# Spreading two products' additions, and fixing VectorE's and TensorE's order, in a decoder trunk on one core

## Chip, cores, metric

The kernel runs on one core of a Trainium2 chip. The metric is the time of one execution on the device in microseconds; the median of three runs of the kernel before is 2475.07 (2474.70 to 2475.67). Engines are named as in the profile: PE is TensorE's matmul, PEld its weight load, DVE VectorE, ACT ScalarE, POOL GpSimd, SP SyncE, whose queue issues most of the DMAs.

## Reference

Two layers: sliding-window attention, then a chunked spatial gating unit (SGU); behind each a conv-gated feed-forward (FFN). Every one of the four is wrapped in norms. The input is 1024 tokens of 1024 columns, in float32. The change touches the last matrix product of both FFNs and of the SGU, and the input projection of the FFN:

```python
def conv_gated_ffn(h, w_in, conv_w, conv_b, w_out):
    g, u = jnp.split(h @ w_in, 2, axis=-1)
    gp = jnp.pad(g, ((0, 0), (CONV_WIDTH - 1, 0), (0, 0)))
    g = conv_b + sum(conv_w[k] * gp[:, k:k + S] for k in range(CONV_WIDTH))
    return (jax.nn.gelu(g) * u) @ w_out
...
x = x + RMSNorm_post(sublayer(RMSNorm_pre(x)))
```

## The kernel before, in words

All matmuls are in float32 accuracy out of three passes over split operands: each operand is a high part, which ACT makes by a cast, and a low part, which DVE makes by a subtraction (`split`: L808 and L602, tile `osum`, eight buffers). A product of two split operands takes hi·hi, hi·lo and lo·hi.

`out_phase` (L908) ends each FFN and the SGU. The activations `ad` stand in DRAM, and the output is cut into four quarters c00, c01, c10, c11 (tiles `acc`). The quarters are computed by Strassen's seven products in Winograd's form, in two groups: g1 with products P1, P2, P6, P5, P7, P3, P4 of six steps each, and g2 with Q1, Q2, Q6, Q5, Q3, Q7, Q4 of four steps each in the FFNs and five in the SGU. One step is the split of two operands, and twelve matmuls of 128x512 (L880, four banks by three passes). The banks of the products change between `mm` and `ob`/`tb`. Between the products, DVE forms sums of operands (`sums1` to `sums4`) and adds finished products to the quarters; `u1`, `u2`, `u4` collect a running sum of three products (tile `u`, in `ww`) and add it to the quarters as they go.

What is left over of the inner dimension (two chunks) goes in by `part` (L253): its operands are split in Q1 (`chunk`, tile `ohl`, L1032 to L1036), six matmuls go into the bank of each token tile (L259), DVE adds the bank to `acc` (L262), ACT squares `acc` for the norm (L269, `junk`), and DVE multiplies `acc` by the norm's gain in place (L270). Such parts are `c11` in the last step of Q2, `c12` in the last of Q3, `c22` and `c21` in the last of Q7 and Q4. Behind the last three stand the norms.

The order of the work is given by the order of the code, by a scheduler that may move an instruction ahead of others of its engine, and by sections in which an engine keeps the order of the code (`tc.manual_schedule`). `run_products` (L890) strings the steps together. Of each step it first issues the splits of a step further ahead (`AHEAD`), then runs `what` (sums), the matmuls, `more` (a part) and `done` (additions). DVE keeps the code's order in the first 30 steps; from there to the end of the phase the scheduler has its choice on all engines.

In `ffn` (L1099) the input projections of the gated part go by pairs of columns in `pair_chain`: seven products of twelve matmuls (L748), tiles T1 to T4 and hhi/hlo, in three banks, with DVE's additions to `pu`, `u2` (L605) between them. The last pair's second chain is followed by `out_phase`, whose first matmuls the scheduler can place among those of the chain.

Of the kernel before, what the change touches and what calls it, by code (L numbers as in the profile page):

```python
# [37 lines left out]
def trunk_kernel(  # L38
# [27 lines left out]
    def mm_bank():  # L66
        return psum.tile([P, HALF], F32, name="mm", tag="mm")

    def out_bank():
        return pso.tile([P, HALF], F32, name="ob", tag="ob")  # L70
# [81 lines left out]
    def half_of(i):  # L152
        return slice(i * HALF, (i + 1) * HALF)
# [450 lines left out]
    def add_(out, a, b, eng=None):  # L604
        (eng or nc.vector).tensor_tensor(out=out, in0=a, in1=b, op=ALU.add)  # L605
# [111 lines left out]
    def chain(products, p1, u2, u4, a, b, c, out):  # L717


        go = iter(products)  # L720
        next(go)(a, True)
        nc.scalar.copy(out=p1, in_=a)
        yield
        next(go)(b, True)
        add_(u2, b, p1)
        yield
        next(go)(a, False)
        out(0, 0, a, None)
        yield
        next(go)(b, False)  # L730
        add_(u4, b, p1)
        yield
        next(go)(c, True)
        out(1, 1, c, u4)
        yield
        next(go)(b, False)
        out(0, 1, b, p1)
        yield
        next(go)(c, False)
        out(1, 0, c, u2)  # L740
        yield
# [11 lines left out]
    def pair_chain(ws, blocks, out):  # L753

        pu = gainp.tile([P, 2, HALF], F32, name="pu", tag="gpost")
        u2 = gainp.tile([P, 2, HALF], F32, name="u2", tag="gpre")[:, 0]
        a, b, c = out_bank(), mm_bank(), mm_bank()
        yield from chain([pair_product(w, t[1], blocks) for w, t in zip(ws, TERMS)], pu[:, 0], u2, pu[:, 1], a, b, c,
                         out)
# [28 lines left out]
    NPAIR = 6  # L788
# [100 lines left out]

    def run_products(products):  # L890

        steps = [s for p in products for s in p.steps()]
        n = 0

        def go(i0, i1):
            nonlocal n
            for i in range(i0, i1):
                while n < min(i + AHEAD[i >= 7 * NPAIR - 4] + 1, len(steps)):
                    steps[n][0]()
                    n += 1  # L900
                steps[i][1]()

        with tc.manual_schedule(engines={mybir.EngineType.DVE}):
            go(0, 5 * NPAIR)
        go(5 * NPAIR, len(steps))

    def out_phase(nchunk, ad, w_out, make_sub):
        with tc.tile_pool(name="junkp", bufs=2) as junkp:  # L908
# [2 lines left out]
    def out_phase_(nchunk, ad, w_out, make_sub, junkp):  # L911
# [33 lines left out]
        c = {(i, j): [sub.acc[4 * i + t][:, half_of(j)] for t in range(4)] for i in range(2) for j in range(2)}  # L945
# [33 lines left out]
        def both(*fs):  # L979
            def f(b):  # L980
                for x in fs:
                    x(b)
            return f

        def same(p):
            return lambda: p.banks


        def early(first):
# [5 lines left out]
        P5 = Product(g1, "P5", four0, both(g1.late, g1.sums4), less(c[0, 1], c[1, 0]))  # L995
        P7 = Product(g1, "P7", four1, None, both(from_(c[1, 1], c[0, 1]), lambda b: load((0, 1))))
        P3 = Product(g1, "P3", four0, None, add_to(c[0, 1]))
# [4 lines left out]
        g2 = Group(n2, [(xnp, "xn")] * 4 + [(work, "work")] * (n2 - 4), w_block(2 * NPAIR))  # L1002
        spare = halves(hs[0] + hs[1]), halves(soon), halves(hs[2] + hs[3])
        blocks = [("A", 0, 0, 0), ("B", 0, 0, 0), ("B", 0, 1, 1), ("A", 1, 0, 0), ("B", 1, 0, 1), ("B", 1, 1, 0),
                  ("A", 0, 1, 2), ("A", 1, 1, 2)]
# [41 lines left out]
        ww = []  # L1047
# [7 lines left out]
        def u2(b):  # L1055
            for t in range(4):
                add_(ww[t], b[t], ww[t])
                add_(c[1, 0][t], ww[t], c[1, 0][t])

        def u4(b):  # L1060
            for t in range(4):
                sub_(ww[t], b[t], ww[t])
                add_(c[0, 1][t], ww[t], c[0, 1][t])
                add_(c[1, 1][t], ww[t], c[1, 1][t])

        def c11(t, b):
            part(t, 0, b)
# [14 lines left out]
        Q1 = Product(g2, "P1", four0, both(g2.sums1, chunk), u1)  # L1082
        Q2 = Product(g2, "P2", same(Q1), g2.sums2, more=c11, first=False)
        Q6 = Product(g2, "P6", four1, g2.sums3, u2)
        Q5 = Product(g2, "P5", four0, g2.sums4, u4)
        Q3 = Product(g2, "P3", four1, more=c12)
        Q7 = Product(g2, "P7", four0, None, c22)
        Q4 = Product(g2, "P4", same(Q7), more=c21, first=False)
        run_products(seq + [Q1, Q2, Q6, Q5, Q3, Q7, Q4])
        return sub.h  # L1090

    def run(gen, *background):
        for _ in gen:
            poke()
            for b in background:
                next(b, None)


    def ffn(layer, h, make_sub):  # L1099
        nfc = DFF // P  # L1100
# [19 lines left out]
        with tc.tile_pool(name="gsp", bufs=2) as gsp, tc.tile_pool(name="cvp", bufs=4) as cvp:  # L1120

            def part(j, half, parts):
                if half == 0:
                    new_gs(j)
                    gu[j] = in_unit(fw_in[layer], j * P)
                    uu[j] = in_unit(fw_in[layer], DFF + j * P)
                ps = in_proj(gu[j], h, half, parts)
                yield
                nc.scalar.copy(out=gs[j][:, 2 + half * HALF:2 + (half + 1) * HALF], in_=ps)
                cv = cvp.tile([P, HALF], F32, name="cv", tag="cv")  # L1130
                conv(j, cv, half * HALF, HALF)
                ps = in_proj(uu[j], h, half, parts)
                yield
                nc.vector.tensor_tensor(out=cv, in0=ps, in1=cv, op=ALU.mult)
                nc.sync.dma_start(out=ad[j][:, half_of(half)], in_=cv)

            for j in range(2):
                run(part(j, 0, 2))
            flush()
            blocks = Blocks(h)  # L1140
            bs = blocks.steps()
            for j in range(2):
                run(part(j, 1, 2), bs, bs, bs)
            for j in range(2, 2 * PLAIN_FFN):
                for half in range(2):
                    run(part(j, half, 1), bs, bs, bs, bs, bs)
            run(bs)

            def gate(j, first=False):

                cv = {}

                def cv_of(i, jj):
                    return cv[i, jj] if first and i == 0 else cv[i][:, half_of(jj)]

                def g_out(i, jj, ps, rest):
                    dst = gs[j + i][:, 2 + jj * HALF:2 + (jj + 1) * HALF]
                    if rest is None:
                        nc.scalar.copy(out=dst, in_=ps)
                    else:  # L1160
                        add_(dst, ps, rest)
                    if first and i == 0:
                        cv[i, jj] = cvp.tile([P, HALF], F32, name="cv", tag="cv")
                        conv(j, cv[i, jj], jj * HALF, HALF)
                    elif i != jj:
                        cv[i] = work.tile([P, S], F32, name="cv", tag="work")
                        conv(j + i, cv[i], 0, S)

                def u_out(i, jj, ps, rest):
                    dst = cv_of(i, jj)  # L1170
                    if rest is not None:
                        add_(rest, ps, rest)
                        ps = rest
                    nc.vector.tensor_tensor(out=dst, in0=ps, in1=dst, op=ALU.mult)
                    if first and i == 0:
                        nc.sync.dma_start(out=ad[j][:, half_of(jj)], in_=dst)
                    elif i != jj:
                        nc.sync.dma_start(out=ad[j + i], in_=cv[i])

                return g_out, u_out  # L1180

            j0 = 2 * PLAIN_FFN
            g_out, u_out = gate(j0, True)
            gw = pair_unit(fw_in[layer], j0 * P, (j0 + 1) * P, True)
            new_gs(j0)
            new_gs(j0 + 1)
            gc = first_chain(gw, blocks, g_out, cvp.tile([P, HALF], F32, name="p1", tag="cv"))
            next(gc)
            next(gc)
            uw = pair_unit(fw_in[layer], DFF + j0 * P, DFF + (j0 + 1) * P, True)  # L1190
            uc = first_chain(uw, blocks, u_out, cvp.tile([P, HALF], F32, name="p1", tag="cv"))
            next(uc)
            for _ in gc:
                pass
            for _ in uc:
                pass

            for j in range(j0 + 2, nfc, 2):
                g_out, u_out = gate(j)
                gw = pair_unit(fw_in[layer], j * P, (j + 1) * P)  # L1200
                new_gs(j)
                new_gs(j + 1)
                run(pair_chain(gw, blocks, g_out))
                uw = pair_unit(fw_in[layer], DFF + j * P, DFF + (j + 1) * P)
                run(pair_chain(uw, blocks, u_out))

        return out_phase(nfc, ad, fw_out[layer], make_sub)

# [259 lines left out]
```

## Time and profile before

| | us |
|---|---|
| median of three runs | 2475.07 |
| the profiled execution, whole | 2475.61 |
| its span in the trace | 2473.9 |
| PE busy | 2414.4 (98%) |
| DVE busy | 1851.3 (75%) |
| ACT busy | 1052.4 (43%) |
| POOL busy | 341.8 (14%) |

Times of the trace count from the start of the span. The first FFN's last product runs from about 780 to 1000, the SGU's from 1560 to 1790, the second FFN's from 2225 to the end. Busy shares are means; a wait in the views of waits is put down to the release that came last.

### The profile page before, as it was taken

The page shows a single profiled execution, that of the slowest core. Times are in us where ns is not written, and L with a number is a line of the kernel's source. Part 1 is how long each engine was busy: PE and PEld are TensorE (multiplying, and loading weights), DVE is VectorE, ACT ScalarE, POOL GpSimd, SP SyncE. Part 2 cuts the span into 40 slices and gives each one's busy share as a digit, 9 for nine tenths or more (in the row PEclk, how much of TensorE's full clock was granted, in tenths as well). Part 3 has the DMA queues.
Part 4 walks back from the last instruction along what each step waited for, and adds up shares of the span by engine and source line. Part 5 has one row for each costly group of instructions (what it writes and reads, how often), then busy time and mean ns, then how long its engine had stood idle before and what let it go on. Part 6 is the DMA issues. An engine that isn't in the chain of part 4 may idle for free.

```text
span 2473.9 us, 33879 instructions
## 1 busy us (share of the span) xinstructions
PE 2414.4 (98%) x12488; PEld 2029.6 (82%) x12488; DVE 1851.3 (75%) x3224; ACT 1052.4 (43%) x1957; POOL 341.8 (14%) x442
## 2 busy tenths in 40 slices
PE   9999989999999999999999999999999999999997
PEld 8777778888887787789998888788797888887886
DVE  5766799767767887886667776787887767767877
ACT  4654565333333444443333333444453333334443
POOL 1000010000000111100027777202110000001011
PEclk9999999999999999999999999999999999999999
DMA  7322142222224952433334444974222222238642
GB/s 238 65 47 56 44 154 69 77 87 92 69 94 154 260 156 69 153 107 99 94 97 148 135 141 150 295 220 81 94 95 85 68 94 86 76 103 259 192 86 102
DMA packets 269943, 296.34 MB, mean 120 GB/s; under 512 B 30447, under 2 KB 195665, under 8 KB 269778
## 3 DMA queue, kind: packets, MB, share of 16 engines
q1 hardware_dynamic: 257106, 271.11, 34.2%
q0 software_dynamic: 12672, 23.07, 5.7%
q8 instruction: 98, 1.61, 0.3%
q14 instruction: 67, 0.55, 0.1%
HBM read 211.29 MB, written 65.01 MB: 112 GB/s over the span
## 4 chain that ended last, share of the span: by engine, by line
PE 84%; DVE 10%; DMA 3%; issue 2%; ACT 1%; POOL 0%; SPq 0%; DVEq 0%; POOLq 0%; ACTq 0%
PE mm L748 27%; PE ob L748 11%; PE mm L880 11%; PE mm L148 7%; PE mm L1286 6%; PE ob L880 3%; PE ob L259 3%; PE tb L880 3%; PE ob L1286 2%; DVE osum L602 2%; PE tb L1416 2%; DMA raw<-ad 2%; PE mm L259 1%; DMA raw<-in_ffn_w_out 1%; PE tb L473 1%
## 5 line engine op out<-in xcount | busy, mean ns | idle before, releaser
L748 PE MATMUL mm<-T,wsum 128*128 128x512 f32 x2496 | 597.4, 392 | 5.4 <-ACT wsum L710 4.2
L748 PEld LDWEIGHTS mm<-T,wsum 128*128 128x128 f32 x2496 | 468.3, 189 | 105.8 <-ACT wsum L710 6.0
L880 PE MATMUL mm<-osum 128*128 128x512 f32 x1644 | 390.1, 391 | 8.1 <-ACT osum L808 4.4
L880 PEld LDWEIGHTS mm<-osum 128*128 128x128 f32 x1644 | 306.6, 188 | 76.0 <-DVE osum L602 5.8
L808 ACT CAST osum<-raw 128x512 fp32r<-128x512 f32 x372 | 215.8, 619 | 305.2 <-PE mm L880 103.7
L602 DVE TENSOR_TENSOR osum<-raw,osum 128x512 fp32r<-128x512 f32 x372 | 242.9, 690 | 84.2 <-ACT osum L808 84.0
L748 PE MATMUL ob<-hhi,wsum 128*128 128x512 f32 x864 | 287.3, 393 | 0.1
L710 ACT CAST wsum<-sums 128x512 fp32r<-128x512 f32 x208 | 127.7, 621 | 292.8 <-DVE sums L602 164.1
L1401 POOL TENSOR_SCALAR vn<-vn,mv,rv 128x128 f32<-128x128 f32 x192 | 193.3, 1018 | 73.9 <-DMA vn<-vd 26.2
L602 DVE TENSOR_TENSOR wsum<-sums,wsum 128x512 fp32r<-128x512 f32 x208 | 142.8, 690 | 68.0 <-ACT wsum L710 67.5
L748 PEld LDWEIGHTS ob<-hhi,wsum 128*128 128x128 f32 x864 | 161.7, 188 | 35.7 <-ACT wsum L710 3.4
L748 PE MATMUL ob<-hlo,wsum 128*128 128x512 f32 x432 | 168.7, 390 | 0.0
L710 ACT CAST wsum<-raw 128x512 fp32r<-128x512 f32 x156 | 96.5, 620 | 163.7 <-PE mm L748 140.3
L605 DVE TENSOR_TENSOR pu<-mm,pu 128x512 f32<-128x512 f32 x110 | 75.7, 688 | 105.4 <-PE mm L748 105.3
L880 PE MATMUL ob<-osum 128*128 128x512 f32 x480 | 133.8, 393 | 13.8 <-DVE osum L602 13.8
L148 PE MATMUL mm<-hhi,whi 128*128 128x256 f32 (+1 forms) x416 | 136.0, 329 | 0.7 <-ACT hhi L211 0.7
L148 PE MATMUL mm<-hlo,whi 128*128 128x256 f32 (+1 forms) x416 | 135.7, 327 | 0.0
L148 PE MATMUL mm<-hhi,wlo 128*128 128x256 f32 (+1 forms) x416 | 134.6, 325 | 0.2 <-DVE wlo L125 0.2
L880 PE MATMUL tb<-osum 128*128 128x512 f32 x480 | 132.5, 389 | 0.0
L748 PE MATMUL mm<-hhi,wsum 128*128 128x512 f32 x384 | 126.7, 391 | 0.0
L1116 DVE SCALAR_TENSOR_TENSOR cv<-gs,cw,cv 128x1024 f32<-128x1024 f32 (+1 forms) x100 | 115.7, 1157 | 14.1 <-issue 8.3
L880 PEld LDWEIGHTS ob<-osum 128*128 128x128 f32 x480 | 88.9, 188 | 38.0 <-DVE osum L602 20.2
(257 smaller groups left out, 4526.6 us busy)
## 6 DMA issues: line engine op xcount, KB each, us to landing
raw<-in_ffn_w_in SPq DMA_DIRECT2D x88, 512.0 KB, 4.0
raw<-ad SPq DMA_DIRECT2D x80, 256.0 KB, 5.4
raw<-in_ffn_w_out SPq DMA_DIRECT2D x80, 256.0 KB, 5.7
ad<-cv SPq DMA_DIRECT2D x38, 512.0 KB, 3.2
raw<-in_sgu_w_in SPq DMA_DIRECT2D x28, 512.0 KB, 4.4
xs<-xt SPq DMA_DIRECT2D x24, 512.0 KB, 2.6
vn<-vd SPq DMA_DIRECT2D x48, 256.0 KB, 3.2
ads<-ut SPq DMA_DIRECT2D x24, 512.0 KB, 3.1
```

Source lines behind the costliest of these rows:

```text
L148: nc.tensor.matmul(ps[:, cs], a[:, k, :], b[:, k, cs], start=n == 0, stop=n == 3 * KC - 1)
L259: nc.tensor.matmul(ps, a, b[:, half_of(nh)], start=n == 0 and not begun, stop=n == end, skip_group_check=begun)
L602: (eng or nc.vector).tensor_tensor(out=out, in0=a, in1=b, op=ALU.subtract)
L605: (eng or nc.vector).tensor_tensor(out=out, in0=a, in1=b, op=ALU.add)
L710: nc.scalar.copy(out=t[:, 0], in_=src)
L748: nc.tensor.matmul(bank, x, y, start=first and n == 0, stop=n == 3 * H4 - 1, skip_group_check=True)
L808: nc.scalar.copy(out=t[:, 0], in_=src)
L880: nc.tensor.matmul(self.banks[t], u, v, start=self.first and g == 0 and m == 0, stop=last and self.more is None and m == 2, skip_group_che ...
L1116: nc.vector.scalar_tensor_tensor(out=cv, in0=gs[j][:, k + t0:k + t0 + n], scalar=tap_w(k, j), in1=cv, op0=ALU.mult, op1=ALU.add)
L1286: nc.tensor.matmul(bank[r][:, q * NQ:(q + 1) * NQ], x, y, start=first and q == 0 and m == 0, stop=m == 3 * H4 - 1, skip_group_check=True)
L1401: nc.gpsimd.tensor_scalar(out=vn[:, t, :], in0=vn[:, t, :], scalar1=mv[:, tt, 0:1], scalar2=rv[:, tt:tt + 1], op0=ALU.subtract, op1=ALU.mult)
L1416: nc.tensor.matmul(sv[:, t, :], vn[:, t, :], gws[(j + i) // 3][0], start=True, stop=True)
```

## The change

Three things. (1) `u2` and `u4` only update the running sum; its additions to the quarters, `plus_u`, are `what` of later products: one token tile in each of four steps of Q5 (to c10), Q3 (to c01) and Q7 (to c11). (2) DVE keeps the order of the code up to the last step of Q3: 61 of 70 steps in an FFN, 66 of 77 in the SGU. (3) The last `pair_chain` of the up-projection of each FFN keeps the code's order on PE.

```diff
     def run_products(products):
...
+        fixed = len(steps) - 2 * products[-1].group.n - 1
         with tc.manual_schedule(engines={mybir.EngineType.DVE}):
-            go(0, 5 * NPAIR)
-        go(5 * NPAIR, len(steps))
+            go(0, fixed)
+        go(fixed, len(steps))
...
         def u2(b):
             for t in range(4):
                 add_(ww[t], b[t], ww[t])
-                add_(c[1, 0][t], ww[t], c[1, 0][t])
 
         def u4(b):
             for t in range(4):
                 sub_(ww[t], b[t], ww[t])
-                add_(c[0, 1][t], ww[t], c[0, 1][t])
-                add_(c[1, 1][t], ww[t], c[1, 1][t])
+
+        def plus_u(i, j):
+
+            return lambda t: add_(c[i, j][t], ww[t], c[i, j][t]) if t < 4 else None
...
-        Q5 = Product(g2, "P5", four0, g2.sums4, u4)
-        Q3 = Product(g2, "P3", four1, more=c12)
-        Q7 = Product(g2, "P7", four0, None, c22)
+        Q5 = Product(g2, "P5", four0, both(plus_u(1, 0), g2.sums4), u4)
+        Q3 = Product(g2, "P3", four1, plus_u(0, 1), more=c12)
+        Q7 = Product(g2, "P7", four0, plus_u(1, 1), c22)
...
                 uw = pair_unit(fw_in[layer], DFF + j * P, DFF + (j + 1) * P)
-                run(pair_chain(uw, blocks, u_out))
+                with tc.manual_schedule(engines={mybir.EngineType.PE}) if j + 2 >= nfc else ExitStack():
+                    run(pair_chain(uw, blocks, u_out))
```

The changed code's lines count from one more behind L891 to four more at the end (L1035 is L1037). In the rows of the order below, the numbers behind a name are those of its buffer or tile.

DVE in the first FFN, before, around the c11 parts, which stand in the last step of Q2. `acc_7333` to `acc_7336` are the four token tiles of c11, `osum_8408` and `osum_8411` the operands of a step of Q6:

```order
L602 TENSOR_TENSOR osum_8389<-sums_7341,osum_8389 128x512
L262 TENSOR_TENSOR acc_7333<-mm_8256,acc_7333 128x512
L270 TENSOR_TENSOR acc_7333<-acc_7333,gpost_7263 128x512
L275 TENSOR_SCALAR ms_8759<-ss2_8451 128x1
L262 TENSOR_TENSOR acc_7334<-mm_8257,acc_7334 128x512
L262 TENSOR_TENSOR acc_7335<-mm_8258,acc_7335 128x512
L270 TENSOR_TENSOR acc_7334<-acc_7334,gpost_7263 128x512
L275 TENSOR_SCALAR ms_8790<-ss2_8465 128x1
L602 TENSOR_TENSOR osum_8408<-raw1_7275,osum_8408 128x512
L602 TENSOR_TENSOR osum_8411<-sums_7342,osum_8411 128x512
L262 TENSOR_TENSOR acc_7336<-mm_8259,acc_7336 128x512
L270 TENSOR_TENSOR acc_7335<-acc_7335,gpost_7263 128x512
```

The same place of the change, where `osum_8432` and `osum_8435` are Q6's third step and `acc_7336` to `acc_7339` the four tiles; `osum_8498` and `osum_8501`, Q6's last step, are the next row behind these:

```order
L602 TENSOR_TENSOR raw1_7278<-sums_7347,raw1_7278 128x512
L262 TENSOR_TENSOR acc_7336<-mm_8258,acc_7336 128x512
L270 TENSOR_TENSOR acc_7336<-acc_7336,gpost_7266 128x512
L262 TENSOR_TENSOR acc_7337<-mm_8259,acc_7337 128x512
L275 TENSOR_SCALAR ms_8758<-ss2_8453 128x1
L270 TENSOR_TENSOR acc_7337<-acc_7337,gpost_7266 128x512
L262 TENSOR_TENSOR acc_7338<-mm_8260,acc_7338 128x512
L275 TENSOR_SCALAR ms_8789<-ss2_8467 128x1
L270 TENSOR_TENSOR acc_7338<-acc_7338,gpost_7266 128x512
L262 TENSOR_TENSOR acc_7339<-mm_8261,acc_7339 128x512
L275 TENSOR_SCALAR ms_8832<-ss2_8481 128x1
L270 TENSOR_TENSOR acc_7339<-acc_7339,gpost_7266 128x512
```

Before, splits stand between the tiles, and two L262 ahead of the second L270. Now the four tiles follow each other, each with its L270 behind its own L262 and ahead of the next tile's, and no split lies between them.

ACT at the same place, before (L269 is the square, L808 the cast of a split):

```order
L808 CAST osum_8389<-sums_7341 128x512
L269 ACTIVATE junk_8443,ss2_8451<-acc_7333 128x512
L269 ACTIVATE junk_8457,ss2_8465<-acc_7334 128x512
L808 CAST osum_8408<-raw1_7275 128x512
L808 CAST osum_8411<-sums_7342 128x512
L269 ACTIVATE junk_8471,ss2_8479<-acc_7335 128x512
L269 ACTIVATE junk_8485,ss2_8493<-acc_7336 128x512
L808 CAST osum_8430<-raw1_7275 128x512
L808 CAST osum_8433<-sums_7343 128x512
L808 CAST osum_8496<-raw1_7275 128x512
```

ACT, the change:

```order
L808 CAST osum_8435<-sums_7346 128x512
L808 CAST osum_8498<-raw1_7278 128x512
L808 CAST osum_8501<-sums_7347 128x512
L808 CAST osum_8521<-sums_7344 128x512
L808 CAST osum_8524<-raw1_7278 128x512
L269 ACTIVATE junk_8445,ss2_8453<-acc_7336 128x512
L269 ACTIVATE junk_8459,ss2_8467<-acc_7337 128x512
L269 ACTIVATE junk_8473,ss2_8481<-acc_7338 128x512
L269 ACTIVATE junk_8487,ss2_8495<-acc_7339 128x512
```

The first two squares have moved behind eight more casts; the last four of these are of Q6's last step (`osum_8498`, `osum_8501`) and of Q5's first (`osum_8521`, `osum_8524`).

PE in the last up-projection of the first FFN, before (`T1` and `T3` are tiles of operands, `mm_7023` the bank of this half's product and `mm_7161` that of another):

```order
L748 MATMUL mm_7023<-T1_4435,wsum_7002 128x512 x2
L748 MATMUL mm_7023<-T1_4436,wsum_7002 128x512
L748 MATMUL mm_7023<-T1_4435,wsum_7002 128x512
L748 MATMUL mm_7161<-T3_4504,wsum_7147 128x512 x2
L748 MATMUL mm_7161<-T3_4505,wsum_7147 128x512
L748 MATMUL mm_7161<-T3_4504,wsum_7147 128x512
L748 MATMUL mm_7023<-hhi1_3741,wsum_7010 128x512
L748 MATMUL mm_7023<-hlo1_3742,wsum_7010 128x512
L748 MATMUL mm_7023<-hhi1_3741,wsum_7010 128x512 x2
```

PE there, the change:

```order
L748 MATMUL mm_7023<-T1_4436,wsum_7002 128x512
L748 MATMUL mm_7023<-T1_4435,wsum_7002 128x512 x2
L748 MATMUL mm_7023<-T1_4436,wsum_7002 128x512
L748 MATMUL mm_7023<-T1_4435,wsum_7002 128x512
L748 MATMUL mm_7023<-hhi1_3741,wsum_7010 128x512
L748 MATMUL mm_7023<-hlo1_3742,wsum_7010 128x512
L748 MATMUL mm_7023<-hhi1_3741,wsum_7010 128x512 x2
L748 MATMUL mm_7023<-hlo1_3742,wsum_7010 128x512
```

The four matmuls of T3 that stood between the last of T1 and the first of hhi, into another bank, are gone from there; T3's twelve now come further down, one after the other.

## Rows read from the trace of the kernel before

**Rows 1.** The page: busy us, share of the span, instructions.

```profile
PE 2414.4 (98%) x12488; PEld 2029.6 (82%) x12488; DVE 1851.3 (75%) x3224; ACT 1052.4 (43%) x1957; POOL 341.8 (14%) x442
```

**Rows 2.** Waits of PE, whole span: us in total, times, longest.

```profile
PE ob L880 <- DVE osum L602: 13.8, 15, 1.7
```

**Rows 3.** Waits of PE, 950 to 976 us, Q5 and Q3.

```profile
PE ob L880 <- DVE osum L602: 2.3, 2, 1.7
PE mm L880 <- DVE osum L602: 0.5, 1, 0.5
```

**Rows 4.** Timeline of DVE near Q6: start, us, what [idle before <- releaser].

```profile
936.42 0.69 DVE L262 TENSOR_TENSOR acc<-mm,acc 128x512 f32<-128x512 f32 x1 [0.39 <-PE mm L259]
937.96 0.69 DVE L270 TENSOR_TENSOR acc<-acc,gpost 128x512 f32<-128x512 f32 x1 [0.85 <-ACT junk L269]
...
938.64 0.68 DVE L262 TENSOR_TENSOR acc<-mm,acc 128x512 f32<-128x512 f32 x1
...
945.24 0.69 DVE L602 TENSOR_TENSOR osum<-raw,osum 128x512 fp32r<-128x512 f32 x1 [0.42 <-ACT osum L808]
```

**Rows 5.** Timeline of ACT, the same stretch.

```profile
937.21 0.63 ACT L269 ACTIVATE junk<-acc 128x512 f32<-128x512 f32 x1 [2.64 <-DVE acc L262]
...
950.55 0.61 ACT L808 CAST osum<-raw 128x512 fp32r<-128x512 f32 x1
```

**Rows 6.** Timeline of PE, Q6 of the first FFN and of the SGU.

```profile
941.66 1.52 PE L880 MATMUL ob<-osum 128*128 128x512 f32 x6
...
951.64 1.07 PE L880 MATMUL tb<-osum 128*128 128x512 f32 x4
...
1716.46 1.07 PE L880 MATMUL ob<-osum 128*128 128x512 f32 x4
```

**Rows 7.** Timelines, Q6 of the SGU: DVE, then ACT.

```profile
1711.58 0.69 DVE L602 TENSOR_TENSOR osum<-sums,osum 128x512 fp32r<-128x512 f32 x1
...
1713.62 0.62 ACT L808 CAST osum<-sums 128x512 fp32r<-128x512 f32 x1
...
1716.28 0.61 ACT L808 CAST osum<-sums 128x512 fp32r<-128x512 f32 x1
```

**Rows 8.** DMA issues: KB each, median us to landing.

```profile
raw<-ad SPq DMA_DIRECT2D x4, 512.0 KB, 4.6
```

**Rows 9.** Waits of PE, 980 to 1085 us, norms after the first FFN.

```profile
PE tb L210 <- DVE t L602: 2.9, 1, 2.9
PE ob L1286 <- DVE vlo L602: 1.6, 1, 1.6
PE mm L880 <- DVE acc L602: 1.1, 1, 1.1
```

**Rows 10.** Timelines, last up-projection: first FFN (PE, DVE), second (PE).

```profile
777.88 0.50 PE L748 MATMUL mm<-hhi,wsum 128*128 128x512 f32 x1
...
793.76 0.74 PE L880 MATMUL mm<-osum 128*128 128x512 f32 x2 [1.98 <-ACT osum L808]
...
777.14 0.69 DVE L605 TENSOR_TENSOR pu<-mm,pu 128x512 f32<-128x512 f32 x1 [2.50 <-PE mm L748]
...
788.95 1.28 DVE L1116 SCALAR_TENSOR_TENSOR cv<-gs,cw,cv 128x1024 f32<-128x1024 f32 x1
...
2237.77 0.74 PE L880 MATMUL mm<-osum 128*128 128x512 f32 x2 [1.90 <-ACT osum L808]
```

**Rows 11.** Stretches: us, busy us of each engine, granted clock, DMA, GB/s.

```profile
425.00:430.80 5.80, 3.38 (x12) 1.62 (x11) 5.80 (x9) 4.39 (x8) 0.00 (x0) 1.00 0.31 90
430.80:434.40 3.60, 3.60 (x10) 2.81 (x11) 3.41 (x7) 1.69 (x4) 0.00 (x0) 0.53 0.03 9
...
1062.30:1069.20 6.90, 5.66 (x15) 4.33 (x16) 6.90 (x10) 2.28 (x4) 0.00 (x0) 0.51 0.01 2
...
790.00:797.00 7.00, 5.02 (x22) 3.79 (x21) 3.51 (x6) 2.29 (x3) 0.00 (x0) 1.00 0.85 296
966.00:976.00 10.00, 7.70 (x33) 5.69 (x32) 8.47 (x15) 2.81 (x5) 0.00 (x0) 1.00 0.29 105
```

## The prediction

> **What bounds the kernel now.** I read the page first, for its busy shares [rows 1]. TensorE (PE) is busy for 2414.4 us, 98% of the span, and VectorE (DVE) for 75%, so the end is set by PE, and only what opens or closes a gap on PE counts. Second, the view of PE's waits, for who ends those gaps [rows 2]: the largest is "ob L880 <- DVE osum L602", 13.8 us in 15 waits, a matmul waiting for the low half of a split operand. Third, the same view for the stretch that the change aims at, Q5 and Q3 in the first FFN: 0.5 + 2.3 = 2.8 us [rows 3]. The same stretch of the SGU and of the second FFN prints the same two rows, so spreading the additions can win 8.4 us at the very most. Fourth, the timelines of DVE, ACT and PE around Q6, where the fixed order puts something new: [rows 4 to 6]. There the reader should see that the c11 parts' chains (L262, ScalarE's square L269, L270) begin at 936.42, a tile at a time, while PE goes on with Q6 at 941.66 without a gap.
>
> The profiled execution took 2475.61 us; the median of the runs is 2475.07. I add to the first and take off 0.5 at the end. About 5 us (0.2%) is what a measurement of this kernel can tell from no change.
>
> **1. The c11 parts, now in fixed order.** Before, each L262, L270 and split ran on DVE when it was ready: two tiles, then a split, then the rest. In the fixed order all four tiles stand in one row behind the low halves of Q6's third step, each L270 straight behind the L262 of its own tile, and the splits of Q6's fourth step stand behind all of them. L270 overwrites what the square reads, so DVE stands still until the square is done. One tile costs, from the start of one L262 to the start of the next, 938.64 − 936.42 = 2.22 us [rows 4]; without the tiny L275, which moves into the waiting time, 2.15. The square itself also moves: on ACT the four squares now stand behind the casts of Q6's last and Q5's first step. The second of those casts starts at 950.55 and takes 0.61 [rows 5]; it waits for PE's third step, which is not earlier than before.
>
> So: first square at 951.16; L270 follows 937.96 − 937.21 = 0.75 later and takes 0.61 at DVE's cadence: 952.5. Three more tiles, 3 × 2.15: 959.0. Then two low halves, 0.61 + 0.69: 960.3. PE needs them after the high passes of two steps, which the order interleaves, at 951.64 [rows 6]. PE stands for **8.7 us**; queued behind the four tiles on DVE are the splits of Q6's last and all of Q5's steps, and PE alone waits for those. The loads of Q5's operands on SP's and POOL's queues wait for buffers that come free as late as PE is, and are ahead of it by the same distance: nothing. The second FFN has the same order and the same durations: **8.7**. In the SGU one square is ahead of the casts of the step after: its first cast row is at 1713.62 and ends at 1714.23 [rows 7], the first L262 is done at 1714.6 (it starts behind the three additions that follow the low half at 1711.58: 1712.2 + 1.8 = 1714.0), its L270 at 1716.05. The second square waits for two more casts, of which the later starts at 1716.28, so the second L270 ends at 1718.3; two more tiles, 1722.6; two low halves, 1723.9. PE needs them at 1716.46 [rows 6]: **7.5 us**. Sum: 24.9. Bounds: nothing, if DVE stands while PE still has work (which would need the chain to be done by 950.3), and 4 × 2.22 + 1.3 = 10.2 in each phase.
>
> **2. The additions of U2 and U4, spread.** Taken out: 2.8 us in each phase [rows 3]. But in Q3 DVE must now do one acc addition and one sums4 addition ahead of each split. Two additions are 1.22, and cast and low half take 0.61 + 0.61 + 0.69 = 1.9 from the release of a buffer: 3.1 us of chain for a step of 2.72. That leaves 0.4 in each of four steps, and I put 0.9 on the step in which the four subtractions of U4 come as well: 2.5 per FFN phase, −0.3 each. The SGU's Q3 has one step more in which the splits can run ahead, so I put 0.95 there: −1.85. Together **−2.45**; bounds −8.4 (every gap gone) and +2.
>
> **3. Q1.** ACT's cast of Q1's second chunk (L1035) now stands ahead of the split casts of the next step. Its 512 KB load lands a median 4.6 us after issue [rows 8], and is issued only after the first chunk's subtraction. I estimate 0.4 in each FFN phase and nothing in the SGU: **+0.8**; bounds 0 and 4.6 × 2 less what lies beside, some +3.6.
>
> **4. The norms.** The additions of c10, c01 and c11 that left Q5 come later, into Q3 and Q7. Eight at 0.61 with four more of sums4 are up to 7 us of DVE work pushed towards the norms, where PE waits for DVE already [rows 9]: 2.9 + 1.6 + 1.1 after the first FFN. Part of it lies beside Q7 and Q4 (eight steps of 2.72). I take 2.4 us (four additions) as the most that arrives late, and 1.5, 1.0 and 0.5 as estimates in the three phases (after the second FFN PE's rest is short): **+3.0**; bounds 0 and 7.2.
>
> **5. The last up-projection in fixed order.** Removed are the gaps of 1.98 and 1.90 [rows 10], in which PE waits for the cast of an operand of P1 whose matmuls had been drawn into the chain. Put in their place: T1, the hi/lo twelve and T4 stand back to back. The twelve write T1's bank and wait for DVE's pu, which ran from 777.14 to 777.83; PE went on at 777.88 without a gap [rows 10] because four matmuls of T3 (0.91) stood between. They are gone from there: about 1.0 of new wait. At the second half the same wait comes behind a cv of 1.28 on DVE [rows 10]: 1.4 as an estimate. 2.4 against 1.9 is +0.5 each, **+1.0**; bounds −3.9 (no new gap) and +3.
>
> **6. The clock.** Where PE had worked 3.38 of 5.80 us, the next 3.60 ran at a granted clock of 0.53 [rows 11]; the longest such stretch is 6.90 us at 0.51 [rows 11]. That is 1.2 GHz in place of 2.4. In each new stall PE works far less than that (at most eight matmuls in 9 us). A stretch of 3.60 us at 0.53 loses 0.47 × 3.60 = 1.7; one behind each of three stalls is **+5.1**. Bounds: 0 and 3 × 0.49 × 6.90 = 10.1.
>
> The Trainium skill, "TensorE: Matmul & The Clock Gate", section "A second HAM failure mode: psum-queue depth-cycling", says that small, frequent idles between groups of matmuls are enough to make the clock fall and rise again and again; that speaks against part 2, which makes two large gaps into four or five small ones. By that rule Q3 would lose one more stretch in each phase, 3 × 1.7 = 5.1. Here the row 966 to 976 has PE at 7.70 of 10 us, with the gaps in it, at 1.00 [rows 11], so the trace of before does not bear it out.
>
> Sum: 2475.6 + 24.9 − 2.45 + 0.8 + 3.0 + 1.0 + 5.1 = 2508.0; on the scale of the median **2507.5**.
>
> **The rivals.**
> *The clock stays up.* The rest of the sum holds, without 5.1: 2502. For it: 1.98 us of idle at 793.76 left the clock at 1.00 [rows 10, 11].
> *More of the clock.* Each stall is followed by the long stretch, or the small gaps of Q3 drop it: +5.1 again, 2513. This is where the rule of the Trainium skill in part 6 would lead, if Q3 were the place.
> *The chain costs half.* The squares get in between the casts (ACT's order is a queue, but its casts may be released earlier), so that DVE's own cadence, 1.22 a tile, sets it: 4 × 0.93 = 3.7 less in each phase, and no clock: 2502 less 11, near 2491; if the first square also stands ahead of the casts, it starts 2.2 earlier (the first L262 would be done at 949.0), 2484.
> *Faster.* L270 of the fourth tile is through by 950.3, so PE never waits, and only the gains are left: part 2's −2.45, part 5 without new gaps −3.9, part 3's +0.8: 2475.1 − 5.5 = 2469.5. It decides at 950.3: the chain of four would have to begin near 941.7. Against it: the low halves of the third step, behind which it stands, start at 945.24 [rows 4].
> *No effect*, if the order of DVE were not the limit anywhere: 2475.
>
> **How the numbers follow.** The forecast, 2504 to 2511: 0.50. Clock stays up, 2498 to 2504: 0.22. More of the clock, 2511 to 2518: 0.12. Half the chain, 2482 to 2494: 0.08. Faster, 2470: 0.04. No effect or something near it: 0.04. From 2490 to 2515 lie the first two whole, about three quarters of the third and some of the fourth: a little over 0.8. Faster by over 0.2%: 0.03, since 2470 lies at that bound; within 0.2%: 0.05; slower: 0.92.
>
> **What would show it.** In the profile after: one wait of PE for "DVE osum L602" of about 8 us in each of the three phases, near Q6's fourth step; on DVE there four pairs of L262 and L270 in a row with an idle "<- ACT junk L269" ahead of each L270; on ACT the squares behind the casts; a granted clock of 0.5 right after the stall. In Q3, four or five gaps of about 0.5 in place of 1.70 and 0.60. No gap of 1.9 at the last up-projection, but some 2 us of waits for DVE's pu. I am wrong if PE passes Q6 without a wait of over 2 us.

## The result, and the profile after

The changed kernel takes 2507.34 us (2506.45 to 2508.29), the kernel before in the same session 2475.37: the ratio is 1.0130, with a 95% interval of 1.0117 to 1.0143. It is slower by 32 us. The forecast was 2507.5. The profiled execution took 2507.93 us, its span is 2506.2.

The page after, where [rows 1] stood:

```profile
span 2506.2 us, 33928 instructions
PE 2430.0 (97%) x12488; PEld 2035.8 (81%) x12488; DVE 1856.0 (74%) x3224; ACT 1052.3 (42%) x1957; POOL 338.8 (14%) x442
```

The number of matmuls is the same, and PE is *busy* for 15.6 us more than before, so part of the loss does not show as waiting. Two things are in these 15.6 us: matmuls at half the clock, which take longer, and matmuls that stand alone between two waits, which the trace counts at 0.5 to 0.8 us each, where one in a row takes 0.227. How much is the clock is worked out below.

The view of PE's waits, whole span (us in total, times, longest), where [rows 2] stood:

```profile
PE ob L880 <- DVE osum L602: 20.2, 15, 7.5
PE mm L880 <- DVE acc L262: 6.1, 4, 1.6
...
PE mm L880 <- DVE ms L275: 3.0, 2, 1.6
```

The longest wait for a low half went from 1.7 to 7.5 us, and two names are new, which PE's L880 did not wait for before: PE waits for the banks that L262 reads. (In the rows with "ms L275" the matmul also waits for L262, which ends just behind that small instruction's start.) Where they lie shows in DVE's timeline of the first FFN at Q6, columns as in [rows 4]:

```profile
946.97 0.69 DVE L602 TENSOR_TENSOR raw<-sums,raw 128x512 f32<-128x512 f32 x1
947.58 0.68 DVE L262 TENSOR_TENSOR acc<-mm,acc 128x512 f32<-128x512 f32 x1
950.88 0.69 DVE L270 TENSOR_TENSOR acc<-acc,gpost 128x512 f32<-128x512 f32 x1 [2.62 <-ACT junk L269]
951.49 0.68 DVE L262 TENSOR_TENSOR acc<-mm,acc 128x512 f32<-128x512 f32 x1
...
952.96 0.69 DVE L270 TENSOR_TENSOR acc<-acc,gpost 128x512 f32<-128x512 f32 x1 [0.73 <-ACT junk L269]
...
957.24 0.69 DVE L270 TENSOR_TENSOR acc<-acc,gpost 128x512 f32<-128x512 f32 x1 [0.79 <-ACT junk L269]
957.85 0.68 DVE L602 TENSOR_TENSOR osum<-raw,osum 128x512 fp32r<-128x512 f32 x1
```

and in PE's beside it:

```profile
948.97 0.73 PE L880 MATMUL ob<-osum 128*128 128x512 f32 x2
...
950.28 0.50 PE L880 MATMUL mm<-osum 128*128 128x512 f32 x1
952.23 0.49 PE L880 MATMUL mm<-osum 128*128 128x512 f32 x1 [1.45 <-DVE acc L262]
954.31 0.80 PE L880 MATMUL mm<-osum 128*128 128x512 f32 x1 [1.59 <-DVE acc L262]
956.45 0.79 PE L880 MATMUL mm<-osum 128*128 128x512 f32 x1 [1.34 <-DVE ms L275]
959.19 2.07 PE L880 MATMUL ob<-osum 128*128 128x512 f32 x4 [1.95 <-DVE osum L602]
```

DVE stands ahead of each L270 for the square of the same tile: 2.62 us for the first, which stands on ACT behind the casts, and 0.73 and 0.79 for the next ones; between the first L262 and the split it stands for 4.9 of 10.3 us. The split behind the four tiles begins at 957.85, and PE goes on with the low halves at 959.19, 10.22 us after it began the step's high ones at 948.97. Between the two it has the high passes of two steps to do, eight matmuls at 2.72 / 12 = 0.227 us, 1.8 in all: the stall is 8.4 us. The second of these two steps writes the banks that L262 empties one by one, so its four matmuls (at 950.28 to 956.45) come one at a time, and PE has four waits. The second FFN shows the same waits. The SGU has one wait in place of four:

```profile
1738.56 2.08 PE L880 MATMUL ob<-osum 128*128 128x512 f32 x4 [7.50 <-DVE osum L602]
```

The four matmuls behind each stall take 2.07 and 2.08 us, against 1.07 for four in [rows 6]. The stretches (columns as in [rows 11]) say why:

```profile
959.20:964.50 5.30, 5.30 (x13) 4.14 (x14) 2.04 (x5) 1.14 (x2) 0.00 (x0) 0.50 0.00 0
1738.60:1742.70 4.10, 4.10 (x10) 3.24 (x11) 1.17 (x3) 0.33 (x1) 0.00 (x0) 0.50 0.00 0
2426.10:2432.20 6.10, 6.08 (x14) 4.79 (x15) 2.53 (x5) 1.14 (x2) 0.00 (x0) 0.50 0.00 0
```

PE is busy all through, at a granted clock of 0.50 (1.2 GHz in place of 2.4). Half of 5.3 + 4.1 + 6.1 is 7.8 us; with the stalls of 8.4, 7.5 and 8.4 that is 32.1.

Where the time went, by the start of the n-th of PE's 12488 matmuls in the two traces, in us:

```
n-th matmul, place                    before     after    later by
 4000  ahead of last up-projection    767.64    766.33    -1.31
 4700  end of Q2, first FFN           932.10    931.10    -1.00
 4800  Q5, behind the stall           955.04    965.20    10.16
 4900  Q3                             981.41    991.14     9.74
 9000  Q2 of the SGU                 1695.37   1709.81    14.44
 9100  Q6, behind the stall          1718.05   1741.71    23.66
 9200  Q3                            1743.54   1764.88    21.34
12200  Q6, second FFN                2390.91   2412.81    21.90
12300  Q3, behind the stall          2416.37   2448.28    31.92
12487  the last but one              2461.33   2493.78    32.45
```

Of 32.45 us, 11.2 + 9.2 + 10.0 = 30.4 arise in the three short stretches that hold the c11 tiles; 4.7 between the first FFN's Q3 and the SGU's Q2, where the norms are; and 2.3 are won in the SGU's Q5 and Q3.

### The profile page after: what moved, and what is told of

It is laid out like the page before. It is cut to its first block, busy times and chain, and to the rows that moved or that the text cites. A ratio compares the mean times of both kernels' runs of the same rounds, so it can differ in the third digit from the quotient of the medians.

```text
span 2506.2 us, 33928 instructions
## 1 busy us (share of the span) xinstructions
PE 2430.0 (97%) x12488; PEld 2035.8 (81%) x12488; DVE 1856.0 (74%) x3224; ACT 1052.3 (42%) x1957; POOL 338.8 (14%) x442
## 4 chain that ended last, share of the span: by engine, by line
PE 85%; DVE 10%; ACT 2%; issue 2%; DMA 1%; POOL 0%; SPq 0%; DVEq 0%; POOLq 0%; ACTq 0%
PE mm L748 27%; PE mm L880 12%; PE ob L748 11%; PE mm L148 7%; PE mm L1290 6%; PE ob L259 4%; PE ob L880 3%; PE tb L880 3%; PE ob L1290 2%; DVE osum L602 2%; PE tb L1420 2%; PE mm L524 1%; PE mm L259 1%; PE tb L473 1%; PE mm L514 1%
## 5 line engine op out<-in xcount | busy, mean ns | idle before, releaser
L880 PE MATMUL mm<-osum 128*128 128x512 f32 x1644 | 393.8, 393 | 13.3 <-DVE acc L262 6.1
L880 PEld LDWEIGHTS mm<-osum 128*128 128x128 f32 x1644 | 308.7, 189 | 85.2 <-DVE acc L262 7.3
L808 ACT CAST osum<-raw 128x512 fp32r<-128x512 f32 x372 | 215.6, 619 | 320.8 <-PE mm L880 106.1
L602 DVE TENSOR_TENSOR osum<-raw,osum 128x512 fp32r<-128x512 f32 x372 | 242.1, 685 | 101.2 <-ACT osum L808 100.8
L602 DVE TENSOR_TENSOR wsum<-sums,wsum 128x512 fp32r<-128x512 f32 x208 | 142.2, 688 | 71.8 <-ACT wsum L710 71.2
L880 PE MATMUL ob<-osum 128*128 128x512 f32 x480 | 138.4, 403 | 21.8 <-DVE osum L602 20.2
L880 PE MATMUL tb<-osum 128*128 128x512 f32 x480 | 135.5, 395 | 0.0
L880 PEld LDWEIGHTS ob<-osum 128*128 128x128 f32 x480 | 89.9, 192 | 49.9 <-DVE osum L602 26.7
```

The costliest lines, as they stand in the source:

```text
L808: nc.scalar.copy(out=t[:, 0], in_=src)
L880: nc.tensor.matmul(self.banks[t], u, v, start=self.first and g == 0 and m == 0, stop=last and self.more is None and m == 2, skip_group_che ...
```

## The experiments

In the front part "c11" is the name of a function: its parts go to the quarter that the code calls c[0, 0]. The diffs show the main lines of each edit; "..." marks what is left out. Where a run's code is longer, its line numbers are higher than those above (L885 is L880, L607 is L602, L1294 is L1286). "The trace, matmul by matmul" means a table like the one above, of one profiled execution of each kernel. The theory: the loss is the row of four c11 tiles in VectorE's fixed order, in which L270 waits for the square of its own tile. Each run is compared with runs of the kernel before on the same chip.

**Parts of the change, alone.** First, part 3 only:

```diff
-                run(pair_chain(uw, blocks, u_out))
+                with tc.manual_schedule(engines={mybir.EngineType.PE}) if j + 2 >= nfc else ExitStack():
+                    run(pair_chain(uw, blocks, u_out))
```

> Only part 3 of the change (TensorE's fixed order in the last up-projection). The theory, that the loss is the row of four c11 tiles on VectorE: no stall at Q6, the gaps of 1.98 and 1.90 us become 0.78 + 0.89 us twice as in the changed kernel, the time is within 1 us of before: 2475. The rival, that TensorE's order takes part in the loss: over 2480.

Measured: 2471.44, ratio 0.9979 (0.9970 to 0.9988). No stall at Q6, as the theory has it, but 5 us less, not the same. The gain does not lie where part 3 acts: of the 5.1 us between the two traces, matmul by matmul, the last up-projection of the first FFN wins 0.1. By 450 us, ahead of the first instruction that stands elsewhere, 1.3 are won, then 3.2 between 1048 and 1090 us and 0.7 between 1868 and 1885. PE's waits from 1060 to 1085 us, before and in this run:

```profile
PE tb L210 <- DVE t L602: 2.9, 1, 2.9
PE ob L1286 <- DVE vlo L602: 1.6, 1, 1.6
PE tb L1434 <- ACT t L219: 0.9, 1, 0.9
```

```profile
PE tb L210 <- DVE t L602: 2.9, 1, 2.9
PE tb L1435 <- ACT t L219: 0.6, 1, 0.6
```

At the start of the SGU, 270 us further on, the scheduler has put other instructions ahead of each other, and a wait of 1.6 us is gone; from 1062 to 1069 us the mean granted clock is 0.76, where it was 0.51 [rows 11]. A fixed stretch also changes what the scheduler makes of the stretches behind it.

Then parts 1 and 3, with `fixed = 5 * NPAIR`:

> Parts 1 and 3, with VectorE's order free from step 30 on as before. The theory: no wait of TensorE above 2.5 us in Q6, no half-clock stretch there, time 2470 to 2477. The rival, that the spread additions are what comes late: 2480 or more, with waits in Q5 and Q3.

Measured: 2471.91, ratio 0.9980 (0.9970 to 0.9989). No stall. Spreading the additions adds nothing to part 3 as long as the order is free: in the two traces all engines show the same sequence of operations and tile names, so the scheduler puts the spread additions back to where they were. Then part 2 only:

```diff
-            go(0, 5 * NPAIR)
-        go(5 * NPAIR, len(steps))
+            go(0, len(steps) - 2 * products[-1].group.n - 1)
+        go(len(steps) - 2 * products[-1].group.n - 1, len(steps))
```

> Part 2 alone (VectorE in fixed order up to the norms, additions of U2 and U4 at once as before). The theory: the same stalls at Q6 as in the changed kernel, some 8.4, 7.5 and 8.4 us, with the clock's 5 to 8 us behind them, so 2505 to 2515 whatever Q3 adds. The rival: under 2490.

Measured: 2524.26, ratio 1.0192 (1.0177 to 1.0207). The stalls are there, and the time lies above the range. In the first FFN's Q5 and Q3, 965 to 1000 us, PE now waits:

```profile
PE mm L880 <- DVE osum L602: 2.2, 1, 2.2
PE ob L880 <- DVE osum L602: 2.0, 1, 2.0
PE mm L880 <- DVE u L602: 1.4, 1, 1.4
```

The fixed order that holds up c11 holds up U2's and U4's additions too: U4's four subtractions and eight additions stand in one row on DVE ahead of Q3's splits. Two more stretches at half clock follow these waits in this phase (974.5 and 991.6). So part 2 alone costs 48 us, and with parts 1 and 3 it costs 32: these two are worth some 16 us together once the order is fixed. How much of that is the spreading alone was not run; part 3 by itself gave 5 us with a free order.

**The gain multiply put off.** In the changed kernel, `part` gives c11's L270 to a list, and each step of Q6 takes one:

```diff
...
-        Q6 = Product(g2, "P6", four1, g2.sums3, u2)
+        Q6 = Product(g2, "P6", four1, both(g2.sums3, gain), u2)
```

> The changed kernel, with only the gain multiply (L270) of the four c11 tiles put off, one into each step of Q6. VectorE keeps its fixed order and the splits still stand behind the four L262. The theory (L270 waits for the square, tile by tile): the four L262 cost 2.4 us in a row, TensorE waits about 0.5 us in the FFNs and 1.3 in the SGU, no half-clock stretch, time 2476 to 2479. The rival (the fixed order makes the splits late whatever the square does): waits of over 4 us stay, time over 2490.

Measured: 2482.17, ratio 1.0022 (1.0012 to 1.0031). Twenty-six of the 32 us are gone. DVE at the same place, and PE's only wait in the SGU's Q6, 1710 to 1732 us:

```profile
949.02 2.48 DVE L262 TENSOR_TENSOR acc<-mm,acc 128x512 f32<-128x512 f32 x4
951.42 0.68 DVE L607 TENSOR_TENSOR osum<-raw,osum 128x512 fp32r<-128x512 f32 x1
```

```profile
PE ob L885 <- DVE osum L607: 1.4, 1, 1.4
```

Four L262 now run back to back in 2.4 us, and the 1.4 us are what was expected of them there. The time is 3 us above the range: matmul by matmul, 5.9 us are lost in the norms behind the first FFN, and at most 1.8 at Q6 in any phase. The fixed order with the splits behind four L262 is nearly harmless; the tile-by-tile wait for the square, with the multiply behind it, is what cost.

**Chain earlier.** The chain as it is, but the splits of Q6's second and third steps issued behind it (`hold` is the number of Q2's last step):

```diff
-                while n < min(i + AHEAD[i >= 7 * NPAIR - 4] + 1, len(steps)):
+                while n < min(i + AHEAD[i >= 7 * NPAIR - 4] + 1, len(steps) if i > hold else hold + 2):
...
+        hold = len(steps) - 5 * products[-1].group.n - 1
```

> The changed kernel with the chain of L262, square and L270 as it is, but the splits of Q6's second and third steps issued behind it instead of ahead of it. The theory (the four tiles wait on VectorE behind splits whose buffers PE frees only a step and a half later, and that is why their 8.6 us lie open): the chain now starts near 936 as in the kernel before and runs beside PE's own c11 matmuls, what stays open is 1 to 2 us in each phase for the low half behind it, no half-clock stretch, 2482 to 2488. The rival (four serial tiles cost their 8.6 us wherever they stand): over 2500.

Measured: 2510.29, ratio 1.0143 (1.0128 to 1.0158). Here I was wrong: the time is the rival's, although the chain did not come to where the theory wanted it. DVE's timeline, and PE's stall:

```profile
938.55 0.68 DVE L602 TENSOR_TENSOR sums<-raw 128x512 f32<-128x512 f32 x1
...
942.05 0.69 DVE L602 TENSOR_TENSOR raw<-sums,raw 128x512 f32<-128x512 f32 x1
942.66 0.68 DVE L262 TENSOR_TENSOR acc<-mm,acc 128x512 f32<-128x512 f32 x1
944.68 0.69 DVE L270 TENSOR_TENSOR acc<-acc,gpost 128x512 f32<-128x512 f32 x1 [1.33 <-ACT junk L269]
```

```profile
952.99 2.07 PE L880 MATMUL ob<-osum 128*128 128x512 f32 x4 [9.28 <-DVE osum L602]
```

With the splits out of the way the first L262 begins at 942.66 in place of 947.58, not at 936.4, because the sums2 subtractions of Q2's steps, which the free order had done by 918.5, now stand in code order ahead of it. So the splits were only part of what made the chain late. And what is won there is lost again, since PE now needs the splits behind the chain one step sooner: it stands still for 9.28 us. Whether a chain that begins at 936 would hide beside PE's work, this run does not show. Both cures together (the cap, and L270 put off):

> Both cures: the four gain multiplies put off into Q6's steps, and the splits of Q6's second and third steps behind the four L262. The theory: no wait of PE over 0.5 us in Q6 in any phase; against the run with the deferral alone 1 to 3 us less, 2479 to 2481; what is left above the kernel before lies in the norms.

Measured: 2488.05, ratio 1.0049 (1.0034 to 1.0064): a second miss. With the cap even four L262 leave a wait of 2.7 us in each FFN, where the run without the cap has none, so issuing splits late does harm by itself.

**Q3 and the norms.** With both cures, `both(g2.sums4, plus_u(1, 0))` in place of `both(plus_u(1, 0), g2.sums4)`:

> As the run with both cures, and in Q5 the sums4 addition stands ahead of the quarter's addition, so that the cast of Q3's operand is released 0.6 us earlier. The theory (Q3's small gaps, 4 x 0.22 and 0.69 us, are cast and low half behind two additions): the gaps by ScalarE's cast go in the FFNs, 1 to 3 us less in all. The rival (the buffer that PE frees sets them): no change.

Measured: 2487.96, ratio 1.0048 (1.0033 to 1.0063). It tells nothing in the time; in its trace Q3's small waits are smaller and the norms are worse by as much. With both cures, sums4 in Q6 and both of U4's additions in Q3:

> As the run with both cures, with the sums4 additions moved from Q5 to Q6 and U4's additions to the last quarter from Q7 to Q3. The theory that what is left above before is VectorE's work pushed into the norms: Q3's gaps go, and 2 to 5 us less in the norms behind the first FFN and the SGU: 2470 to 2475. The rival: it comes back as waits in Q6, no better than the run with both cures.

Measured: 2480.39, ratio 1.0019 (1.0010 to 1.0029): 8 us under the run with both cures (4.4 between the two traces), but not under the kernel before: the cap's wait of 2.7 us is still in it. Of the 4.4 us, 3 arise in the first FFN's Q5 and Q3 and only 0.7 in the norms behind it, so the run says that the additions cost in Q3; that they are what costs in the norms it does not show.

**The stretch that holds c11 left free.** The changed kernel, with the stretch from step 30 to Q2's last step in free order and Q6, Q5 and Q3 fixed (`hold` is the number of Q6's first step):

```diff
+        hold = len(steps) - 5 * products[-1].group.n
...
-            go(0, fixed)
-        go(fixed, len(steps))
+            go(0, 5 * NPAIR)
+        go(5 * NPAIR, hold)
+        with tc.manual_schedule(engines={mybir.EngineType.DVE}):
+            go(hold, fixed)
+        go(fixed, len(steps))
```

> The changed kernel with one stretch of VectorE's order left free again: from step 30 of each phase to the last step of Q2, which holds the c11 tiles; Q6, Q5 and Q3 stay in fixed order. The theory (c11 in the fixed order is the whole loss): no wait over 1 us in Q6, no half-clock stretch there, Q5's and Q3's waits smaller than in the kernel before, 2468 to 2475. The rival (fixed order in Q6 to Q3 costs by itself): over 2480.

Measured: 2476.49, ratio 1.0002 (0.9994 to 1.0011). The whole loss is gone by one edit, with all three parts of the change in force elsewhere. The stretch holds more than c11; that c11's chain is what counts in it rests on the run with L270 put off. PE has no wait in Q6 in any phase, and no half clock there. The time is 1.5 us above the range I gave, since the norms take back what Q3 wins: matmul by matmul, Q5 and Q3 win 0.4, 2.8 and 1.5 us in the three phases, and the norms behind the first FFN cost 5.6. PE's waits from 990 to 1100 us, whose first and third rows stand in [rows 9] with 2.9 and 1.6, while the second is new:

```profile
PE tb L210 <- DVE t L602: 2.9, 1, 2.9
PE tb L210 <- DVE hlo L212: 2.5, 1, 2.5
PE ob L1294 <- DVE vlo L602: 1.8, 1, 1.8
```

The same, with sums4 in Q6 and both of U4's additions in Q3:

```diff
-        Q6 = Product(g2, "P6", four1, g2.sums3, u2)
-        Q5 = Product(g2, "P5", four0, both(plus_u(1, 0), g2.sums4), u4)
-        Q3 = Product(g2, "P3", four1, plus_u(0, 1), more=c12)
-        Q7 = Product(g2, "P7", four0, plus_u(1, 1), c22)
+        Q6 = Product(g2, "P6", four1, both(g2.sums3, g2.sums4), u2)
+        Q5 = Product(g2, "P5", four0, plus_u(1, 0), u4)
+        Q3 = Product(g2, "P3", four1, both(plus_u(0, 1), plus_u(1, 1)), more=c12)
+        Q7 = Product(g2, "P7", four0, None, c22)
```

> As the run with the free stretch up to Q2, with the sums4 additions in Q6 and both of U4's additions in Q3, so that less is left for VectorE behind Q3. The theory: Q3's waits of 2.3 us go, 2 to 5 us under the kernel before: 2466 to 2472. The rival (what is won in Q3 comes back in the norms): no faster than the run with the free stretch alone.

Measured: 2470.27, ratio 0.9974 (0.9964 to 0.9984). This beats both kernels. Q5 and Q3 have no wait left in this trace, where [rows 3] had 2.8 us, and matmul by matmul they win about 3 us in each of the three phases; the norms behind the first FFN take 5 us back. Does it need the fixed order? The same places, with the order free from step 30:

> The same places of the additions as in the fastest run (sums4 in Q6, both of U4's in Q3), but VectorE's order free from step 30 on as in the kernel before. If the places of the additions make the gain in Q3, the waits of 2.3 us go here too: 2466 to 2472. If it is the fixed order of Q6 to Q3 that keeps the additions at their places, the scheduler draws them ahead of the splits again, Q3's waits stay at 1.7 and 0.6 us, and the time is that of the run with parts 1 and 3: 2471 to 2476.

Measured: 2471.87, ratio 0.9984 (0.9975 to 0.9993). From 950 to 980 us its waits are those of before, to the digit:

```profile
PE ob L880 <- DVE osum L602: 2.3, 2, 1.7
PE mm L880 <- DVE osum L602: 0.5, 1, 0.5
```

So the place of the additions in the code does nothing while the scheduler may move them: all engines show the sequence of the run with part 3 alone once more, and 2471.44, 2471.91 and 2471.87 are, as far as the traces tell, the time of one order, measured three times. It takes the fixed order and the new places together to take Q3's waits away. What that is worth in time stays open: the interval of the fastest run (0.9964 to 0.9984) overlaps with all three of these, so it is not shown to be faster than part 3 alone.

**The clock.** The changed kernel, with 32 matmuls of a zero operand in Q6's last step; they add zero to the banks:

```diff
...
+                            if m == 0 and last and self.name == "P6" and n < NPAIR:
+                                for _ in range(8):
+                                    nc.tensor.matmul(self.banks[t], zero[0], cb[:, 0], start=False, stop=False,
+                                                     skip_group_check=True)
```

> The changed kernel, with 32 matmuls of a zero operand added to the banks of Q6's last step behind the high passes (7.25 us of TensorE work that adds nothing to the sums), so that TensorE works while it would stand. The theory (the half clock behind the stalls costs 15.6 us at half speed, that is 7.8): the stalls' end does not move, the clock stays at full speed, 2498 to 2501. The rival (the clock is not what lengthens the rows behind the stalls): 2507 or more.

Measured: 2512.31, ratio 1.0145 (1.0132 to 1.0159), and the time alone would speak for the rival. The rows don't. In the first FFN the stall's end stays (PE goes on at 959.77, 10.23 us after the step's start, against 10.22), and the clock is at full speed through and behind it:

```profile
950.00:958.00 8.00, 8.00 (x37) 6.61 (x36) 4.24 (x10) 3.59 (x10) 0.00 (x0) 1.00 0.00 0
...
962.00:966.00 4.00, 4.00 (x19) 3.33 (x18) 2.87 (x5) 2.23 (x4) 0.00 (x0) 1.00 0.00 0
```

Against the changed kernel, this stretch is 2.4 us shorter, and the same one of the second FFN 2.8; half of 5.3 and of 6.1 is 2.65 and 3.05. In the SGU I put the matmuls in the wrong step: there PE's wait lies one step ahead of Q6's last, so they came behind it and cost their own time, 7.9 us with the half clock:

```profile
1737.16 2.08 PE L880 MATMUL ob<-osum 128*128 128x512 f32 x4 [7.44 <-DVE osum L602]
...
1741.17 2.74 PE L884 MATMUL ob<-osum,zero 128*128 128x512 f32 x8
```

What the clock costs is shown for the two FFNs; for the SGU it is read from the rows at 0.50 only.

## Why the prediction was right

The mechanism and its places were right, and the stalls, which are three quarters of the sum, were right in size. That the sum came within half a us is luck: the clock and the norms cost 2.7 us each more than I had put down, and the additions (2.1), the last up-projection (1.2), the stalls (0.6), Q1 (0.2) and a gain that is not the change's (1.3) made up for it.

*Part 1, the c11 tiles:* forecast 8.7, 8.7 and 7.5; measured 8.4, 8.4 and 7.50. The walk by rows held to 0.3 us: one tile takes 2.1 us from L262 to L262, four of them stand ahead of the split. In the FFNs it is not the one wait that I said would show it, but four, since I had let PE run through the second step's high passes, and their banks come free only with each L262; the last of the four still ends with the split, so the sum is the same. The runs with L270 put off and with the stretch of c11 left free show that it was this chain.

*Part 6, the clock:* forecast 5.1, one stretch of 3.6 us behind each stall; measured 5.3, 4.1 and 6.1 us at 0.50, 7.8 in all. The term was too small by 2.7: each stretch began inside the stall and outlasted it longer than I took from the row before. How long is not fixed, though: with part 2 alone, behind the same waits, PE works 5.2, 4.6 and 2.8 us at 0.50 in the three phases, which would cost 6.3. The rule of the Trainium skill ("TensorE: Matmul & The Clock Gate", section "A second HAM failure mode: psum-queue depth-cycling") that small, frequent idles make the clock fall did not come true here: with four waits of 0.2 us and one of 0.7 in Q3, the stretch is at 1.00.

```profile
970.00:990.00 20.00, 18.42 (x75) 13.41 (x74) 17.42 (x29) 5.63 (x10) 0.00 (x0) 1.00 0.00 1
```

*Part 2, the additions:* forecast −2.45. The rows give −1.2 in the first FFN (0.9 + 0.7 in place of 2.8), −1.4 in the second and −2.0 in the SGU: −4.6. In the FFNs I took 0.4 us a step where it is 0.2.

*Part 3, Q1:* forecast 0.8; matmul by matmul, 0.4 us are lost between matmuls 4600 and 4700 of the first FFN, 0.2 at the same place of the second, and nothing in the SGU. Too small to tell more.

*Part 4, the norms:* forecast 1.5, 1.0 and 0.5. Behind the first FFN, PE's waits are 3.1 us more than before, with one more stretch of 3.4 us at half clock near 1060, so 4.7 us; I had 1.5. The SGU and the second FFN come to about 0.5 each by the table. The direction was right, the first FFN's size was not. That this is DVE's pushed work, as I had reasoned, is not shown: with the additions moved to Q6 and Q3 the same norms still cost 5.0 us, against 5.6 with them in place. In the runs with the order free from step 30 this loss is not there, so it comes with the fixed order; by what, stays open.

*Part 5, the last up-projection:* forecast +1.0. The new waits are there, pu and u, 0.8 and 0.9, in place of 1.98 and of 1.90:

```profile
PE mm L748 <- DVE u L605: 0.9, 1, 0.9
PE mm L748 <- DVE pu L605: 0.8, 1, 0.8
```

Matmul by matmul the net is −0.1 us in each FFN. My second wait (1.4) was too long.

What I did not see: 1.3 us are won ahead of matmul 4000, where the order of all engines is the same in both traces. Of the half-clock stretch at 430.8 in [rows 11] nothing is left in the trace after; another of the same length stands at 339.9. That is not the change's doing: of the two runs with the same order, the one with part 3 alone has its stretch near 340 too, the one with parts 1 and 3 near 430. And part 3, worth 0.1 us at its own place, comes with 5 us elsewhere; 3.2 of them lie where the scheduler has chosen another order.

## What to carry to other kernels

Before an engine's order is fixed, look in the code order for an instruction that waits for another engine's answer to the instruction just ahead of it; each such pair costs the whole round trip, times their number, and everything behind them stands. Move the second of the pair a step further on, or leave that stretch free. And price a stall on TensorE at more than its length: here each 8 us were followed by 4 to 6 us of work at half the clock (3 to 5 with part 2 alone).

## What the runs showed of the hardware that I had not expected

The granted clock fell in the FFNs' stalls although single matmuls ran in them, at 950.28, 952.23, 954.31 and 956.45:

```profile
950.00:954.20 4.20, 1.16 (x3) 0.37 (x2) 2.59 (x6) 1.57 (x5) 0.00 (x0) 1.00 0.00 0
954.20:964.50 10.30, 6.90 (x15) 4.73 (x16) 5.47 (x13) 2.58 (x6) 0.00 (x0) 0.50 0.00 0
```

How much work then ran at half the clock did not go by whether single matmuls ran: here it was 5.3 and 6.1 us in the FFNs and 4.1 in the SGU, where PE stood still for 7.5 us; with part 2 alone, behind the same waits, 4.6 in the SGU and 2.8 in the second FFN. Matmuls with an operand of zeros kept the clock at 1.00 in the same place, in both FFNs.
